# FFN1 of a transformer layer: sums of squares on TensorE, a scale on ScalarE, six g buffers, five chunks and adaLN dots placed one by one

## The chip, the cores and the metric

The kernel runs on one core of a Trainium2 chip. A core has five engines that run at the same time, each through its own queue in order: TensorE (PE in the profile), which multiplies matrices into PSUM; VectorE (DVE), ScalarE (ACT) and GpSimd (POOL), which work on vectors; and SyncE (SP), which issues the DMAs here. Engines wait for one another by semaphores. SBUF holds operands, 128 partitions wide; PSUM has eight banks of 512 float32 columns. The metric is the device time of one execution in microseconds (us), as the median of several runs.

## The reference

One layer of a diffusion transformer works on 512 latent and 256 context tokens of width 1024: a first half-step feed-forward network (FFN1), a token mixer (latent attention and a gated MLP), and a second network (FFN2). Nine rows of modulation come from one product of silu(c) with a wide matrix (adaLN), once for latent tokens and once for context tokens.

```python
def rms_norm(x, w):
    xf = x.astype(jnp.float32)
    y = xf * lax.rsqrt(jnp.mean(xf * xf, axis=-1, keepdims=True) + EPS)
    return (y * w.astype(jnp.float32)).astype(x.dtype)

def modulate(h, shift, scale):
    return h * (1 + scale) + shift

def swiglu(h, w1, w3, w2):
    return (jax.nn.silu(h @ w1) * (h @ w3)) @ w2

def ffn_sublayer(h_in, shift, scale, gate, norm_w, w1, w3, w2):
    h = modulate(rms_norm(h_in, norm_w), shift, scale)
    return h_in + 0.5 * gate * swiglu(h, w1, w3, w2)

# in hybrid_layer; D_MODEL 1024, D_FF 2816
    mx = jnp.split((jax.nn.silu(c) @ w_ada + b_ada)[:, None, :], N_MOD, axis=-1)
    mc = jnp.split((jax.nn.silu(c_ctx) @ w_ada + b_ada)[None, None, :], N_MOD, axis=-1)
    x = ffn_sublayer(x, mx[0], mx[1], mx[2], norm1_w, ffn1_w1, ffn1_w3, ffn1_w2)
    ctx = ffn_sublayer(ctx, mc[0], mc[1], mc[2], norm1_w, ffn1_w1, ffn1_w3, ffn1_w2)
```

## The kernel before

**Layout.** x lies transposed: 128 partitions, 8 slices k of the width, and 768 token columns, which are two halves of 256 latent and 128 context tokens. GA and GB are those halves of 384 columns. All float32 products are done with operands split into a high part (`oph`, `hh`, `gh`: a copy on ScalarE) and a low part (`opl`, `hl`, `gl`: a subtraction on VectorE), and three matmuls (L125 to L127: high by high, high by low, low by high). Every weight tile of 128x512 thus costs one copy and one subtraction (L102, L103).

**Start.** ScalarE squares x slice by slice (`square0`). VectorE adds the eight latent squares up (`add_sq`), one float32 matmul with a matrix of ones (L402) sums over partitions, and the inverse root follows (`rstd_start`, `rstd_end`). Before it, PE broadcasts silu(c) for both kinds of tokens into two double banks (L391, 32 passes), runs four matmuls with constants (L394, `WARM`), and ScalarE copies the broadcasts to `cb` (`put_cb`). The eight context squares are added on GpSimd and summed by L479.

**First loop, k = 0 to 7.** With `nc.ordered` set each engine keeps the order in which the code is written. A pass makes slice k of h: `first_x` (x times scale and inverse root, VectorE), `first_h` (adds the shift and makes the high part, ScalarE), `first_l` (low part, VectorE); in the same pass PE accumulates the up products of f = 0 and 1 for the latent columns (L441) and, some passes later, for the context columns (L434). Two adaLN rows are made on the way: scale by PE (`ada_row` L253, `ada_col` L260), shift by VectorE's dots (`ada_shift`).

**adaLN dots.** The other seven rows are dots on VectorE: 128x1024 weights times `cb`, with an accumulator (L223). There are 80 of them: 48 whose products go to a throw-away tile `junk` (two dots to each loaded half block, latent and context) and 32 which write over the half block (`raw`, one dot each). The throw-away tile shares its buffers (tag s1, two of them) with GpSimd's sum `s1` of each Winograd step. `ada_half` makes all the dots of a half block at once; `ada_step` calls it four times after f = 2 and after f = 3 and three times in each Winograd step, until they are used up.

**FFN1's f loop.** f = 2 and 3 are plain products (`up1`). Then the operands of a Strassen-Winograd scheme are made (blocks T1 to T4), and f = 4 to 21 need seven block products each (`head`, `mid`, `tail`), 84 matmuls of 384 columns. GpSimd makes sums of weights (L571 to L587). The results gh, gl of one f (`g_tile`) are kept until a chunk of them goes through the down product: `after1` calls `down` for the chunks of CHUNKS1, at set values of f, and VectorE adds each result bank, gated, to x (`evac_x` L319, one for the latent and one for the context columns). The last chunk (`last_down`) goes first for GA and then for GB, with the next norm between them.

**What sets the order.** Outside the pinned loop a scheduler that simulates the engines sets the order of each engine's instructions; buffers (three `raw`, two `block` tiles, five operand pairs, g tiles) limit how far work runs ahead. PSUM has two double banks (`big`) and four single ones (`mm`); a Winograd f takes four banks, alternately of one kind and the other, and `down` uses single ones. SyncE issues the loads of all weights in program order.

## Time and profile before

| | us |
|---|---|
| median of three runs | 1217.53 (1213.57 to 1220.31) |
| profiled execution | 1216.12 |
| its span | 1214.0 |
| first matmul of the first loop (L441) starts | 19.79 |
| last split of the first loop's last slice (`hl`, k = 7) starts | 69.68 |
| evacuation of the first down product begins | 150.9 |
| last down product's matmuls of FFN1 end | 593.0 |

The profile counts each engine's busy time; a matmul's busy time includes its pipeline, so that matmuls that follow at 0.17 us each have 0.34 us. A row of the timeline gives start, duration, engine, line, operation and tiles, and in brackets how long the engine had been idle and which instruction ended that. A row of the groups gives line, engine, tiles and shapes, the count, then busy time and mean ns of one, then the idle time before them by releaser. L57 is the wrapper through which the pinned stretch issues its work. "PEclk" is the clock that TensorE was granted, as a share of the full one.

### The profile page before, as it was taken

To read this page: it belongs to the slowest core of one execution; us is meant where nothing else is said; L and a number is where in the kernel's file an instruction comes from. 1 tells how busy PE (TensorE), PEld (TensorE's weight loads), DVE (VectorE), ACT (ScalarE), POOL (GpSimd) and SP (SyncE) were. 2 spreads that over 40 slices of the span, in tenths; PEclk is the share of its full clock that TensorE was granted. 3 is DMA by queue.
4 is the path that set the end of the run, shared out by engine and by line. 5 is a ranking of instruction groups with operands and counts; after the bars stand their busy time and mean duration, and the time that the engine had idled before them with its cause. 6 is when DMAs were issued, how large, how long until landed. Compare 5 with 4: busy or idle time off the path is not lost.

```text
span 1214.0 us, 18922 instructions
## 1 busy us (share of the span) xinstructions
PE 1149.2 (95%) x7042; PEld 1078.5 (89%) x7042; DVE 963.5 (79%) x1699; ACT 545.4 (45%) x1090; POOL 422.6 (35%) x388
## 2 busy tenths in 40 slices
PE   8899799979999999999999999998989999999998
PEld 5689699979999999998888789987888989899997
DVE  7999987897876977667864978759996879787784
ACT  6463312233143143245554549985653535354441
POOL 1102311222032042114426727885761424243320
PEclk9999999989999999999999999998999999999999
DMA  9434343343623723224221220003122332323302
GB/s 335 168 125 155 133 145 104 105 170 108 225 75 115 227 75 129 72 87 138 76 100 59 99 66 5 1 1 122 53 71 104 105 105 99 111 73 136 105 35 87
DMA packets 35514, 130.60 MB, mean 108 GB/s; under 512 B 3680, under 2 KB 10592, under 8 KB 29536
## 3 DMA queue, kind: packets, MB, share of 16 engines
q1 hardware_dynamic: 35280, 129.35, 31.3%
q8 instruction: 55, 0.90, 0.3%
q14 instruction: 35, 0.29, 0.1%
q10 hardware_dynamic: 144, 0.06, 0.0%
HBM read 127.30 MB, written 2.10 MB: 107 GB/s over the span
## 4 chain that ended last, share of the span: by engine, by line
PE 70%; DVE 14%; ACT 3%; issue 2%; DMA 1%; POOL 0%; DVEq 0%; POOLq 0%; ACTq 0%
PE mm L125 15%; PE mm L126 15%; PE mm L127 15%; PE big L125 7%; PE big L126 7%; PE big L127 7%; DVE opl L103 4%; DVE junk L223 1%; PE mm L1064 1%; DMA raw<-wada 1%; DVE x L319 1%; DVE hh L301 1%; PE mm L1079 1%; PE mm L1080 1%; DVE hl L302 1%
## 5 line engine op out<-in xcount | busy, mean ns | idle before, releaser
L102 ACT CAST oph<-block 128x512 fp32r<-128x512 f32 x228 | 141.3, 621 | 250.8 <-PE mm L126 167.2
L103 DVE TENSOR_TENSOR opl<-block,oph 128x512 fp32r<-128x512 f32 x228 | 209.3, 922 | 36.4 <-ACT oph L102 35.6
L125 PE MATMUL mm<-gh,oph 128*128 128x384 f32 (+2 forms) x532 | 187.4, 354 | 4.5 <-DVE x L319 4.0
L127 PE MATMUL mm<-gh,opl 128*128 128x384 f32 (+2 forms) x532 | 186.7, 353 | 4.6 <-DVE opl L103 4.6
L126 PE MATMUL mm<-gl,oph 128*128 128x384 f32 (+2 forms) x532 | 187.5, 352 | 0.0
L102 ACT CAST oph<-raw 128x512 fp32r<-128x512 f32 x154 | 94.0, 619 | 145.4 <-PE mm L126 87.1
L587 POOL TENSOR_TENSOR block<-block 128x512 f32<-128x512 f32 x38 | 51.6, 1357 | 258.3 <-DVE opl L103 231.0
L103 DVE TENSOR_TENSOR opl<-raw,oph 128x512 fp32r<-128x512 f32 x154 | 119.2, 779 | 19.6 <-ACT oph L102 19.4
L571 POOL TENSOR_TENSOR s<-block 128x512 f32<-128x512 f32 x38 | 54.7, 1440 | 197.6 <-DVE g L248 75.8
L125 PEld LDWEIGHTS mm<-gh,oph 128*128 128x128 f32 x532 | 100.2, 189 | 12.4 <-issue 4.4
L127 PEld LDWEIGHTS mm<-gh,opl 128*128 128x128 f32 x532 | 100.2, 189 | 12.0 <-DVE opl L103 5.2
L126 PEld LDWEIGHTS mm<-gl,oph 128*128 128x128 f32 x532 | 100.2, 188 | 6.6
L586 POOL TENSOR_TENSOR block<-s,block 128x512 f32<-128x512 f32 x38 | 54.4, 1432 | 121.4 <-DVE opl L103 120.8
L319 DVE SCALAR_TENSOR_TENSOR x<-mm,g,x 128x256 f32<-128x256 f32 x206 | 76.5, 413 | 19.1 <-PE mm L127 19.1
L125 PE MATMUL big<-hh,oph 128*128 128x384 f32 (+1 forms) x240 | 79.8, 333 | 9.6 <-DVE gl L306 7.9
L325 DVE SCALAR_TENSOR_TENSOR x<-mm,g,x 128x512 f32<-128x512 f32 x55 | 41.0, 748 | 50.6 <-PE mm L127 50.4
L126 PE MATMUL big<-hl,oph 128*128 128x384 f32 (+1 forms) x240 | 79.8, 333 | 0.0
L127 PE MATMUL big<-hh,opl 128*128 128x384 f32 (+1 forms) x240 | 79.6, 332 | 0.0
L223 DVE SCALAR_TENSOR_TENSOR junk<-raw,cb 128x1024 bf16<-128x1024 f32 x48 | 63.1, 1315 | 1.7 <-DMA raw<-wada 1.3
L585 POOL TENSOR_TENSOR block<-block 128x512 f32<-128x512 f32 x38 | 60.3, 1588 | 2.8
L127 PE MATMUL mm<-hh,opl 128*128 128x384 f32 x160 | 54.0, 337 | 3.0 <-DVE opl L103 3.0
L126 PE MATMUL mm<-hl,oph 128*128 128x384 f32 x160 | 54.6, 341 | 2.2 <-DVE hl L302 2.2
(500 smaller groups left out, 3390.5 us busy)
## 6 DMA issues: line engine op xcount, KB each, us to landing
raw<-wst SPq DMA_DIRECT2D x82, 512.0 KB, 3.7
block<-wst SPq DMA_DIRECT2D x38, 1024.0 KB, 4.9
raw<-wada SPq DMA_DIRECT2D x56, 512.0 KB, 4.4
block<-wada SPq DMA_DIRECT2D x8, 1024.0 KB, 6.3
x<-xT SPq DMA_DIRECT2D x6, 512.0 KB, 6.7
raw<-wfirst SPq DMA_DIRECT2D x8, 256.0 KB, 5.4
out<-x SPq DMA_DIRECT2D x7, 256.0 KB, 2.2
raw<-wuq SPq DMA_DIRECT2D x2, 384.0 KB, 3.1
```

The costliest lines, as they stand in the source:

```text
L102: self.nc.scalar.copy(dst[0], src)
L103: (eng or self.nc.vector).tensor_sub(dst[1], src, dst[0].bitcast(F32))
L125: nc.tensor.matmul(out, lh, rh, start=first, stop=False, skip_group_check=more)
L126: nc.tensor.matmul(out, lh, rl, start=False, stop=False, skip_group_check=more)
L127: nc.tensor.matmul(out, ll, rh, start=False, stop=last, skip_group_check=more)
L223: nc.vector.scalar_tensor_tensor(out, raw, 1.0, cb[:, which, :], ALU.mult, ALU.mult, accum_out=acc[which][:, c : c + 1] if to is None else to,
L319: nc.vector.scalar_tensor_tensor(x[:, dt, s0 : s0 + sn], pt[:, o : o + sn], mod_g[i][which][:, dt : dt + 1], x[:, dt, s0 : s0 + sn], ALU.m ...
L325: nc.vector.scalar_tensor_tensor(lat(x, dt), two(pt), mod_g[i][0][:, dt : dt + 1], lat(x, dt), ALU.mult, ALU.add)
L571: nc.gpsimd.tensor_add(s1, q[2], q[3])
L585: nc.gpsimd.tensor_sub(q[2], q[0], q[2])
L586: nc.gpsimd.tensor_sub(q[0], s1, q[0])
L587: nc.gpsimd.tensor_sub(q[1], q[1], q[0])
```

## The change

Five edits, all in FFN1:

1. Both sums of squares are accumulated on TensorE, eight float32 matmuls each (`sums`), in place of seven additions on VectorE or GpSimd and one matmul. The four constant matmuls (`WARM`) are gone. The broadcast of c for the context tokens (`put_c(1)`) moves behind `ada_col(0)`, and ScalarE copies each broadcast in two halves.
2. `first_x` is a plain product; the scale is given to the activation in `first_h`.
3. The first loop's latent products use the four single banks, its context products and the small results a double bank each; plain f and Winograd f of FFN1 swap the kind of bank by parity (`in_bigs`), and the first half of the last down uses double banks.
4. Six pairs of g buffers instead of five, five chunks (4, 4, 4, 4, 6) instead of six, whose downs come after f = 5, 9, 13 and 17 instead of after f = 5, 6, 10, 14 and 18.
5. `ada_rest` gives out one dot at a time: four after f = 2 and after f = 3, two in each Winograd step, and eleven in each down, between the evacuations. The throw-away tile is one of its own. The gate's columns are finished one by one.

```diff
-CHUNKS1 = [3, 3, 4, 4, 3, 5]
+CHUNKS1 = [4, 4, 4, 4, 6]
...
+    junk = fp.tile([P, D], BF16, bufs=1, name="junk")
...
-    def ada_dot(raw, c, which, to=None):
...
+    def ada_dot(raw, which, to, last=False):
+        nc.vector.scalar_tensor_tensor(raw if last else junk, raw, 1.0, cb[:, which, :], ALU.mult, ALU.mult, accum_out=to)
...
-    def ada_half(i):
-        r = st.half(wada, i)
-        for which in (0, 1) if i < 5 * NK else (0,):
-            ada_dot(r, i, which)
-            if i % NK == NK - 1:
-                mod_final(i // NK, slice(0, NK), which)
+    def ada_rest():
+        for d in range(NK):
+            r = st.half(wada, 2 * NK + d)
+            for which in range(2):
+                ada_dot(r, which, accg[:, d, which : which + 1])
+                yield
+            nc.vector.tensor_scalar(pairs[0][2][:, d, :], accg[:, d, :], col[:, 2 * NK + d : 2 * NK + d + 1], 0.5, ALU.add, ALU.mult)
+        for i in range(3 * NK, 9 * NK):
+            r = st.half(wada, i)
+            for which in (0, 1) if i < 5 * NK else (0,):
+                ada_dot(r, which, acc[which][:, i : i + 1], i >= 5 * NK)
+                if i % NK == NK - 1:
+                    mod_final(i // NK, slice(0, NK), which)
+                yield
...
-        nc.vector.scalar_tensor_tensor(sel(hf, k), sel(x, k), mod_a[0][which][:, k : k + 1], two(rs[which]), ALU.mult, ALU.mult)
+        nc.vector.tensor_mul(sel(hf, k), sel(x, k), two(rs[which]))
...
-        nc.scalar.activation(sel(hf, k), sel(hf, k), AF.Identity, bias=mod_s[0][which][:, k : k + 1])
+        nc.scalar.activation(sel(hf, k), sel(hf, k), AF.Identity, bias=mod_s[0][which][:, k : k + 1], scale=mod_a[0][which][:, k : k + 1])
...
+    bb = [bigs(2), [mm(), mm()]]
+    pa, sumx = bigs(2)
...
+    def sums(which, sq, k):
+        n = parts[which][1]
+        pin(nc.tensor.matmul(sumx[:, :n], ones, sq, start=k == 0, stop=k == NK - 1))
+
+    put_c(0)
     for k in range(NK):
-        sa = add_sq(sa, k, square0(0, k), nc.vector)
...
+        sums(0, square0(0, k), k)
+    copy_c(0)
...
     ada_col(row, 0)
+    put_c(1)
...
-    pbs = bigs(4)
-    pcs = []
-    sx = None
+    pbs = [mm() for _ in range(2 * NFIRST)]
+    pcs = bigs(NFIRST)
...
         if k == 0:
+            sqx = [square0(1, j) for j in range(NK)]
+        if k == 1:
             for j in range(NK):
-                sx = add_sq(sx, j, square0(1, j), nc.gpsimd)
-        if k == 1:
-            sumx = mm()[:, :256]
-            pin(nc.tensor.matmul(sumx, ones, sx, start=True, stop=True))
+                sums(1, sqx[j], j)
...
-        pool, bufs = (gp, 3) if f % 5 < 3 else (gp2, 2)
+        pool = gp if f % 6 < 3 else gp2
...
-        pbs, banks = part or ({}, bigs(2 * len(groups)))
+        pbs, banks = part or ({}, [mm() for _ in range(2 * len(groups))] if f % 2 else bigs(2 * len(groups)))
...
-            bigs4 = bigs(4) if f % 2 else None
+            bigs4 = bigs(4) if f % 2 == self.in_bigs else None
...
+    def ada_step(n=1):
+        for _ in range(n):
+            next(ada, None)
 
     def after1(f):
         if f < NPLAIN1:
-            for _ in range(4):
-                ada_step()
+            ada_step(4)
         for ci, n in enumerate(CHUNKS1[:-1]):
-            if f == (5 if ci == 0 else (starts1[ci] + n + 1) // 2 * 2):
-                down(starts1[ci], n, U_DN1 + starts1[ci], [GA, GB], lambda pt, dt, g, gn: evac_x(pt, dt, seg_of(g // 384), 0))
+            if f == starts1[ci] + n + 1:
+                slot = 0
+
+                def ev(pt, dt, g, gn):
+                    nonlocal slot
+                    evac_x(pt, dt, seg_of(g // 384), 0)
+                    slot += 1
+                    ada_step(slot % 3 > 0)
+
+                down(starts1[ci], n, U_DN1 + starts1[ci], [GA, GB], ev)
...
-    Winograd(gp, 384, U_UP1, blocks, g_tile, 1).run(NPLAIN1, after1, ada_step)
+    Winograd(gp, 384, U_UP1, blocks, g_tile, 1, 0).run(NPLAIN1, after1, lambda i: ada_step(i < 2))
```

More of the change, by code (lines that the diff above doesn't have):

```diff
@@ L35 @@
 RAWS = 3
-WARM = 4
 OPS = 5
@@ L160, in layer_kernel @@
     accs = const.tile([P, NK, 2], F32, name="accs")
+    accg = const.tile([P, NK, 2], F32, name="accg")
     epsc = const.tile([P, 1], F32, name="epsc")
@@ L414, in layer_kernel @@
     first_l(0, 0)
-    put_cb(1)
+    copy_c(1)
     for _ in shift:
@@ L488, in g_tile @@
     def g_tile(f):
[L489 to L490 removed]
+        pool = gp if f % 6 < 3 else gp2
+        gt[f] = tuple(pool.tile([P, 768], F32R, tag=t, bufs=3, name=f"{t}_{nc.next_id()}") for t in ("gh", "gl"))
         return gt[f]
@@ L518, in up1, with down @@
         return pbs, banks
-    def down(f0, n, u0, groups, evac, dts=range(NK), cache=None):
+    def down(f0, n, u0, groups, evac, dts=range(NK), cache=None, bank=None):
         us = {} if cache is None else cache
@@ L523, in down @@
             for g, gn in groups:
-                pt = mm()
+                pt = bank() if bank else mm()
                 for fi in range(n):
@@ L612, in tail, with run @@
             g_split(Z, gh[:, n:], gl[:, n:])
-        def run(self, f0, after, step=lambda: None):
+        def run(self, f0, after, step=lambda i: None):
             hd = self.head(f0)
@@ L718, in ev @@
             sa.add(dt, g0)
-        down(starts1[-1], CHUNKS1[-1], U_DN1 + starts1[-1], [(GA, GB)[g]], ev, dts, caches[g])
+        down(starts1[-1], CHUNKS1[-1], U_DN1 + starts1[-1], [(GA, GB)[g]], ev, dts, caches[g], None if g else lambda: last_banks.pop(0))
     sA, sB = SsqAcc(npool, 384, nc.gpsimd), SsqAcc(npool, 384, nc.vector)
     nc.scalar.activation(epsc2, gt[NF - 1][0][:, 767:768].bitcast(F32), AF.Abs_reciprocal_sqrt, bias=epsc, scale=0.0)
+    last_banks = [b for _ in range(4) for b in bigs(2)]
     last_down(0, sA, range(8))
+    assert next(ada, None) is None
     def normA():
@@ L1279, in layer_kernel @@
     blocks = {"B11": B11, "B21": B21, "B22": B22, "T1": T1, "T2": T2, "T3": T3, "T4": T4}
-    Winograd(f2, 256, U_UP2, blocks, g2_tile, 2).run(NPLAIN2, after2)
+    Winograd(f2, 256, U_UP2, blocks, g2_tile, 2, 1).run(NPLAIN2, after2)
     lastu = {}
```

54 lines of the change are left out of this document (14 added, 40 removed).

## The prediction

> **What bounds the kernel now.** The page first: TensorE (PE) is busy for 95% of the span, so an edit to FFN1 gains only where PE stands still inside FFN1. The windows of 20 us show where. A stretch at full rate holds 117 matmuls of 384 columns, 0.171 us apart.
>
> ```profile
> span 1214.0 us, 18922 instructions
> PE 1149.2 (95%) x7042; PEld 1078.5 (89%) x7042; DVE 963.5 (79%) x1699; ACT 545.4 (45%) x1090; POOL 422.6 (35%) x388
> ...
> 20.00:40.00 20.00, 14.61 (x71) 10.55 (x71) 19.72 (x34) 8.31 (x19) 8.87 (x7) 0.91 0.78 292
> ...
> 60.00:80.00 20.00, 18.40 (x106) 15.15 (x106) 19.36 (x40) 15.18 (x31) 0.00 (x0) 1.00 0.43 148
> 80.00:100.00 20.00, 19.10 (x114) 18.78 (x113) 19.63 (x38) 7.65 (x16) 0.00 (x0) 1.00 0.41 134
> 100.00:120.00 20.00, 18.52 (x107) 18.20 (x107) 19.37 (x32) 6.93 (x14) 6.00 (x4) 1.00 0.47 157
> 120.00:140.00 20.00, 17.18 (x96) 16.23 (x95) 20.00 (x29) 6.30 (x11) 7.62 (x5) 1.00 0.37 127
> 140.00:160.00 20.00, 14.72 (x66) 13.76 (x65) 18.17 (x31) 4.24 (x10) 4.07 (x3) 0.83 0.44 163
> 160.00:180.00 20.00, 20.00 (x117) 20.00 (x116) 19.03 (x42) 4.90 (x9) 4.88 (x3) 1.00 0.33 107
> ...
> 200.00:220.00 20.00, 18.54 (x107) 18.25 (x106) 18.81 (x41) 4.43 (x8) 4.21 (x3) 1.00 0.32 106
> ...
> 240.00:260.00 20.00, 12.13 (x59) 11.81 (x59) 20.00 (x32) 4.51 (x10) 6.92 (x5) 0.79 0.56 202
> 260.00:280.00 20.00, 20.00 (x112) 20.00 (x112) 15.12 (x25) 8.27 (x16) 5.48 (x4) 0.96 0.32 106
> ...
> 480.00:500.00 20.00, 18.48 (x106) 17.90 (x105) 14.79 (x37) 4.06 (x8) 1.29 (x1) 1.00 0.34 114
> ...
> 300.00:480.00 180.00, 180.00 (x1040) 180.00 (x1039) 143.04 (x259) 58.23 (x108) 45.81 (x32) 1.00 0.43 139
> ```
>
> Columns: stretch, length, PE, PE loads, VectorE (DVE), ScalarE, GpSimd (POOL), then granted clock. Where PE's count falls, DVE is at 18 to 20 of 20 us: from 60 to 160 and from 240 to 260 DVE is the bound. From 300 to 480 PE runs without a gap, so nothing is to be had there. The two long waits and the chain into the second:
>
> ```profile
> 149.86 0.69 PE L127 MATMUL mm<-gh,opl 128*128 128x384 f32 x1 [3.19 <-DVE opl L103]
> 150.35 0.52 PE L125 MATMUL mm<-gh,oph 128*128 128x384 f32 x1
> 150.67 0.52 PE L126 MATMUL mm<-gl,oph 128*128 128x384 f32 x1
> ...
> 256.00 0.69 PE L125 MATMUL big<-hh,oph 128*128 128x384 f32 x1 [7.87 <-DVE gl L306]
> ...
> 240.32 1.78 DVE junk L223 x2
> ...
> 243.23 1.22 DVE junk L223 x2
> 244.45 2.23 DVE raw L223 x2
> ...
> 253.87 1.14 DVE raw L223 x2
> 255.01 0.48 DVE big L611
> 255.49 0.47 DVE gl L306
> ```
>
> What delays PE is a bunch of adaLN dots (L223) put ahead of a split that PE needs. After each wait matmuls start 0.32 us apart, and the granted clock of those stretches is 0.83 and 0.79.
>
> **The change, part by part.** The rows that price it:
>
> ```profile
> 8.45 1.89 PE L394 MATMUL mm<-ones 128*128 128x256 f32 x8
> 11.96 1.12 PE L402 MATMUL mm<-sq,ones 128*128 128x512 f32 x2 [1.62 <-DVE sq L57]
> 13.02 1.14 PE L253 MATMUL mm<-block,sc 128*2 128x128 f32 x9
> 26.54 9.34 POOL L57 TENSOR_TENSOR sq<-sq,sq 128x256 f32<-128x256 f32 x7 [25.25 <-ACT sq L57]
> 25.93 0.68 DVE L57 TENSOR_TENSOR hl<-hfull,hh 128x512 fp32r<-128x512 f32 x1
> 26.53 1.22 DVE L57 SCALAR_TENSOR_TENSOR junk<-block,cb 128x1024 bf16<-128x1024 f32 x1
> 32.44 1.20 DVE L57 TENSOR_TENSOR hl<-hfull,hh 128x512 fp32r<-128x512 f32 x1
> 33.56 1.74 DVE L57 SCALAR_TENSOR_TENSOR junk<-block,cb 128x1024 bf16<-128x1024 f32 x1
> 35.93 0.70 PE L479 MATMUL mm<-sq,ones 128*128 128x256 f32 x2 [3.90 <-POOL sq L57]
> L223 DVE SCALAR_TENSOR_TENSOR raw<-raw,cb 128x1024 f32<-128x1024 f32 x25 | 32.5, 1301 | 6.4 <-DMA raw<-wada 6.1
> L319 DVE SCALAR_TENSOR_TENSOR x<-mm,g,x 128x256 f32<-128x256 f32 x96 | 45.8, 477 | 12.2 <-PE mm L127 12.2
> L319 DVE SCALAR_TENSOR_TENSOR x<-mm,g,x 128x128 f32<-128x128 f32 x96 | 32.6, 339 | 0.0
> raw<-wada SPq DMA_DIRECT2D x56, 512.0 KB, 4.4
> ```
>
> *Latent sums.* One float32 matmul is two records. L402's take 13.02 − 11.96 = 1.06 us a sum; L394's, with 256 columns, start about 0.21 apart, so 0.43 at 512 and 0.86 a sum. Half of the 32 broadcast passes now stand ahead, so the eight sums can start near 6.5 us and end at 13.4 (0.86) or 15.0 (1.06), against 13.02; they cannot end before the last square, at 11 us, plus one sum, 11.9. So −1.1 to +2.0; I take **+0.5**, since PE goes from one to the next as in L394. The Trainium skill (FP8 and Floating Point Precision, TensorE Precision Notes) has true FP32 as four passes through the array, and TensorE: Matmul & The Clock Gate, Part 1, 215.7 ns between warm matmuls of 512 columns: an estimate of 0.86 us a sum. By the pages this term is +0.5, by L402 alone it is +2.0; L394 agrees with the pages, and no run here shows sums in a row.
>
> *Context sums.* While POOL adds (26.54 to 35.88), DVE's subtract takes 1.20 instead of 0.68 and its dot 1.74 instead of 1.22: some 0.5 us on each of five, 2.5 in all. PE stands 3.90 us for POOL's sum. Instead PE gets 16 records at 0.21, 3.4 us, in pass k=1, just where it waited: it starts the third pass at 31 + 3.4 = 34.4 instead of 36.28, so −1.9. With DVE's 2.5 passed on in full, a little more. Range 0 to −4; I take **−2.5**. first_x loses its scale (about 0.07 us on each of 16, on DVE), which ScalarE's activation takes in at no added instruction; ScalarE is busy for 8 to 15 of 20 us there and has the cover. Without that cover it would cost as many tenths.
>
> *Up to the first down (60 to 160).* Missing matmuls there are 3 + 10 + 21 + 51 = 85 from 80 to 160, 14.5 us, and 1.6 in 60 to 80: 16.1 lost. In the new order f=2's products start already inside the last pass of the first loop, in their own banks:
>
> On PE, end of the first loop after the change (big_742 is the bank of f=2, mm_250 one of the first loop's last pass); before, all of that pass stood ahead of f=2:
> ```order
> L125 MATMUL big_742<-hl,oph_749 128x384
> L126 MATMUL big_742<-hh,opl_751 128x384
> L124 MATMUL big_742<-hh,oph_749 128x384
> L125 MATMUL big_742<-hl,oph_749 128x384
> L443 MATMUL mm_250<-hh,oph_628 128x512
> L126 MATMUL big_742<-hh,opl_751 128x384
> L124 MATMUL big_742<-hh,oph_749 128x384
> ```
> Some 13 matmuls, 2.2 us, are done before PE needs DVE's last split. From that split to the operand of the Y product of f=4, where DVE last holds PE in the new order, DVE has 15 dots (1.22 each, 18.3), 10 weight splits (0.68, 6.8), 16 block splits (0.55, 8.8) and some 30 smaller operations (0.42, 12.6): 46.5 us, an estimate from rows. PE has 231 matmuls there, 39.0 us: 7.5 lost. Gain 16.1 − 7.5 + 2.2 = **−11**, between 0 (DVE's order gives it back) and −16.
>
> *Dots spread singly (200 to 280).* Missing matmuls: 10 + 58 + 5 = 73, 12.5 us, half-rate stretches included. DVE's order at the end of f=6, before:
> ```order
> L223 SCALAR_TENSOR_TENSOR raw_2851,accc<-raw_2851,cb 128x1024
> L605 TENSOR_TENSOR big_1991<-big_1991,u_2389_2390 128x384
> L103 TENSOR_TENSOR opl_2666<-block_2424,oph_2664 128x512
> L223 SCALAR_TENSOR_TENSOR junk_2806,accc<-raw_2803,cb 128x1024
> L609 TENSOR_TENSOR big_1989<-big_1989,u_2389_2390 128x384
> L606 TENSOR_TENSOR big_1991<-big_1991,sl_2369 128x384
> L103 TENSOR_TENSOR opl_2688<-block_2424,oph_2686 128x512
> L223 SCALAR_TENSOR_TENSOR raw_2904,accc<-raw_2904,cb 128x1024
> ```
> and in the same place (the tail of a Winograd f, L604 to L610 being the former L605 to L611) after, f=6:
> ```order
> L604 TENSOR_TENSOR big_1436<-big_1436,u_1910_1911 128x384
> L102 TENSOR_TENSOR opl_2152<-block_1937,oph_2150 128x512
> L605 TENSOR_TENSOR big_1436<-big_1436,sl_1890 128x384
> L608 TENSOR_TENSOR big_1434<-big_1434,u_1910_1911 128x384
> L102 TENSOR_TENSOR opl_2174<-block_1937,oph_2172 128x512
> L309 TENSOR_TENSOR gl_1978<-big_1436,gh_1976 128x384
> ```
> The dots have left the tail; they stand between the evacuations of a down instead. A down of four is 192 matmuls, 33 us; DVE then has 16 × (0.477 + 0.339) = 13.1 us of evacuation, 11 dots at 1.22, 13.4, and 8 splits at 0.68, 5.4: 32 us, with no room for the neighbouring f's work. What DVE falls behind there shows in f=6, where six more dots stand ahead of the tail: I leave 4 us of the 12.5. So **−8.5**, between −12.5 and 0.
>
> *Five chunks, six g buffers, banks.* 480 to 500 misses 11 matmuls, 1.9 us, at a change of stage; a last chunk of six gives each group's evacuation 18 × 0.171 = 3.1 us of PE as cover instead of 2.6. I take **−3** for this and the norm behind it, from +1 (a bank that waits for its evacuation, which PE's next product otherwise hides) to −5. The same weights are loaded, in as many loads. Single banks, the shared junk tile and the gate columns taken one by one (eight operations of a few tenths, in DVE's 46.5) I cost at nothing more.
>
> *Sum:* 0.5 − 2.5 − 11 − 8.5 − 3 = −24.5. Against the profiled run's own 1216.1 that is 1191.6; the median shown is 1.4 higher, so about **1192** beside it (1193.0, less a rounding the terms do not support).
>
> **The rivals.**
> - *Dots wait for their loads* (slower). A load lands 4.4 us after its issue, and three raw buffers also carry down's weights. In the first two downs 4 + 5.5 loads go through them in 33 us, one per 3.5 us, against (4.4 + 4) / 3 = 2.8 if a pair of dots, split by an evacuation, holds its buffer for 4 us. In the last two each dot has a load of its own: 15 loads, one per 2.2 us, against (4.4 + 1.5) / 3 = 2.0. 44 dots stand inside the downs, and DVE has no room there, so each wait is PE's: above 24.5 / 44 = 0.56 us per dot the change loses; at 0.7 it ends at 1192 + 31 = 1223. Against it: 25 such dots from 300 to 480 waited 6.1 us, 0.24 each, and PE lost nothing. 8%.
> - *DVE stays the bound up to the first down*: the order pulls other DVE work forward, and the 11 us are not gained: 1203. 20.00 of 20 us from 120 to 140 speaks for it; 15 dots there instead of 26 against. 12%.
> - *The stall of 248 moves* behind the first down at full size: 1192 + 8.5 = 1200. DVE's 32 of 33 us speaks for it. 13%. Part of it is the clock: after 3.19 us of idling matmuls stood 0.32 us apart for 6 us, some 3 us lost. The Trainium skill (TensorE: Matmul & The Clock Gate, Part 1) lets the clock fall only after an idle window of about 3.4 us: by it a remainder of 3 us would cost no clock and the time would be 1197 instead of 1200; the row at 149.86 disagrees, and the row decides.
> - *All of DVE's stalls go*: −16 and −12.5 instead of −11 and −8.5: 1183. 14%.
> - *The change does not do what it says*: the scheduler, which sets the order, puts dots in pairs again as in f=6; that is the third rival's place and price.
>
> **How the numbers follow.** The forecast, 1186 to 1198, has 48%; the rivals in their order 8, 12, 13 and 14%; the last 5% is small mishaps together, around 1212. Range 1180 to 1208: it holds the forecast and rivals two to four but for a part of the last. Half a per cent, 6 us, is about what can be told from no change. Faster 0.89 (forecast, rivals two to four, 2 of the 5%), same 0.03 (the other 3 of it), slower 0.08 (the first rival).
>
> **What would show it.** In the changed profile: 16 records of sums in pass k=1 and DVE's subtract at 0.68 there; PE's counts from 100 to 160 near 110, none at 66; no wait near 8 us at the end of f=6, and granted clock 1.00 from 200 to 280; dots (L221) with under 0.3 us of idle ahead of them, and PE without waits for evacuations inside downs. It is wrong if PE waits for DVE throughout the four downs, or if a stretch that was full from 300 to 480 shows gaps.

## The result and the profile after

The changed kernel takes 1218.78 us (median of 20 runs, 1215.69 to 1222.08) against 1217.55 for the kernel before: 1.0015 times as long, 95% interval 1.0005 to 1.0024. Forecast were 1192. The profiles show one execution each, of 1220.65 us after and 1216.12 before, so the traces lie 3 us further apart than the medians. The 26 us that were to be gained are not there, although much of what was to bring them did happen, as the windows of 20 us of the changed kernel show.

```profile
span 1218.9 us, 18886 instructions
PE 1161.7 (95%) x7062; PEld 1087.3 (89%) x7062; DVE 947.9 (78%) x1666; ACT 547.3 (45%) x1094; POOL 412.4 (34%) x381
...
100.00:120.00 20.00, 18.19 (x105) 17.87 (x104) 19.93 (x33) 7.48 (x15) 6.89 (x4) 1.00 0.40 138
120.00:140.00 20.00, 17.83 (x93) 17.62 (x94) 18.75 (x30) 7.62 (x15) 6.66 (x5) 0.91 0.35 113
140.00:160.00 20.00, 19.88 (x115) 19.59 (x114) 16.42 (x30) 8.39 (x16) 4.21 (x3) 1.00 0.41 129
...
200.00:220.00 20.00, 17.76 (x99) 17.15 (x100) 19.83 (x30) 6.68 (x14) 11.98 (x7) 1.00 0.31 106
240.00:260.00 20.00, 19.40 (x112) 19.11 (x112) 16.65 (x33) 6.42 (x12) 3.09 (x2) 1.00 0.47 159
280.00:300.00 20.00, 18.08 (x96) 17.76 (x95) 14.97 (x25) 5.22 (x9) 5.42 (x4) 0.91 0.52 176
340.00:360.00 20.00, 16.80 (x89) 16.48 (x89) 14.04 (x27) 4.72 (x9) 2.93 (x2) 0.91 0.49 161
440.00:460.00 20.00, 16.98 (x90) 16.66 (x89) 14.00 (x27) 4.71 (x9) 3.05 (x2) 0.91 0.52 176
...
300.00:480.00 180.00, 170.34 (x958) 168.46 (x957) 137.23 (x253) 55.02 (x103) 40.49 (x28) 0.98 0.42 140
```

The stretch from 140 to 160 has 115 matmuls instead of 66, that from 240 to 260 has 112 instead of 59. But from 300 to 480, where TensorE (PE) had no gap before, 82 of 1040 matmuls are missing, and VectorE (DVE) is not full there: 14 of 20 us in the two worst stretches. Both traces can be laid side by side by the time at which PE starts its n-th matmul of 384 columns (worked out from the two traces, in us; differences of the unrounded times):

| n | before | after | difference |
|---|---|---|---|
| first matmul of the first loop | 19.8 | 25.1 | +5.3 |
| 100 (f = 2) | 97.2 | 100.0 | +2.8 |
| 400 (first down) | 163.5 | 158.4 | −5.2 |
| 1000 (past f = 6) | 280.2 | 266.5 | −13.7 |
| 1500 | 367.0 | 361.8 | −5.1 |
| 2100 | 471.0 | 475.2 | +4.2 |
| 2761 (last one of FFN1's last down) | 590.9 | 595.4 | +4.5 |

(In the table of times before, two entries differ from the trace: the first evacuation begins at 152.9, not 150.9, and the last down's matmuls end at 591.3, not 593.0.)

The change gains 19 us from the first matmul to n = 1000 and gives 18 back by n = 2100. What happens there is seen at the head of the down after f = 13. The timeline of the changed kernel, by queue (SyncE's issues, DVE, PE):

```profile
345.39 0.33 SPq L97 DMA_DIRECT2D raw<-wada  x1
...
345.28 0.08 DVE L221 DVE_READ_ACCUMULATOR raw<-raw,cb 128x1 f32 x1
346.35 0.55 DVE L605 TENSOR_TENSOR mm<-mm,sl 128x384 f32<-128x384 f32 x1
349.41 1.22 DVE L221 SCALAR_TENSOR_TENSOR raw<-raw,cb 128x1024 f32<-128x1024 f32 x1 [2.51 <-DMA raw<-wada]
350.56 0.56 DVE L608 TENSOR_TENSOR mm<-mm,u 128x384 f32<-128x384 f32 x1
351.43 0.55 DVE L309 TENSOR_TENSOR gl<-mm,gh 128x384 fp32r<-128x384 f32 x1
...
348.49 0.34 PE L126 MATMUL mm<-gh,opl 128*128 128x384 f32 x1
352.03 0.69 PE L124 MATMUL mm<-gh,oph 128*128 128x384 f32 x1 [3.20 <-DVE gl L309]
352.51 0.53 PE L125 MATMUL mm<-gl,oph 128*128 128x384 f32 x1
```

A dot ends at 345.36 and frees a raw buffer; the load of another dot is issued at 345.39, 0.03 us later; that dot starts at 349.41, after DVE stood idle for 2.51 us. Behind it in DVE's queue are the last operations of f = 13 (L608, then L309, which reads the bank of its result), and the down's next product needs that bank: PE waits 3.20 us and then matmuls start 0.32 us apart for a while. This dot is the 58th that DVE runs; the program gives out 50 ahead of this down and 11 between its evacuations. So it is one of the down's own dots, which DVE's order has ahead of its place, in the tail of f = 13. The groups show the same over all of FFN1, first before, then after; idle time for loads rises from 1.3 and 7.5 us to 8.0 and 18.4:

```profile
L223 DVE SCALAR_TENSOR_TENSOR junk<-raw,cb 128x1024 bf16<-128x1024 f32 x48 | 63.1, 1315 | 1.7 <-DMA raw<-wada 1.3
L223 DVE SCALAR_TENSOR_TENSOR raw<-raw,cb 128x1024 f32<-128x1024 f32 x32 | 42.7, 1335 | 7.8 <-DMA raw<-wada 7.5
...
L221 DVE SCALAR_TENSOR_TENSOR junk<-raw,cb 128x1024 bf16<-128x1024 f32 x48 | 60.7, 1265 | 8.1 <-DMA raw<-wada 8.0
L221 DVE SCALAR_TENSOR_TENSOR raw<-raw,cb 128x1024 f32<-128x1024 f32 x32 | 42.9, 1340 | 18.7 <-DMA raw<-wada 18.4
```

The second surprise is the start. Timeline of PE, ScalarE and DVE in the changed kernel:

```profile
4.51 3.75 PE L389 MATMUL big<-ident,sc 128*128 128x128 f32 x16 [0.54 <-ACT sc L217]
8.05 8.12 PE L398 MATMUL big<-sq,ones 128*128 128x512 f32 x16
16.95 1.91 PE L248 MATMUL big<-block,sc 128*2 128x128 f32 x16 [0.78 <-ACT r L56]
25.09 0.50 PE L443 MATMUL mm<-hh,oph 128*128 128x512 f32 x1
...
18.90 0.25 ACT L56 COPY row<-big 2x128 f32<-2x128 f32 x1 [2.00 <-PE big L248]
...
19.18 0.69 DVE L56 SCALAR_TENSOR_TENSOR v<-big,r 128x512 f32<-128x512 f32 x1 [2.50 <-ACT row L56]
```

The sums end at 16.2, and DVE's first step of the inverse root (`v<-big,r`) then stands 2.50 us for ScalarE's copy of the adaLN row, which has nothing to do with it but lies in the other half of the same double bank.

### The profile page after: what moved, and what is told of

It reads as the page before. It is cut to its first block, busy times and chain, and to the rows that moved or that the text cites. A ratio compares the mean times of both kernels' runs of the same rounds, so it can differ in the third digit from the quotient of the medians.

```text
span 1218.9 us, 18886 instructions
## 1 busy us (share of the span) xinstructions
PE 1161.7 (95%) x7062; PEld 1087.3 (89%) x7062; DVE 947.9 (78%) x1666; ACT 547.3 (45%) x1094; POOL 412.4 (34%) x381
## 4 chain that ended last, share of the span: by engine, by line
PE 66%; DVE 20%; DMA 6%; ACT 4%; issue 4%; POOL 0%; DVEq 0%; POOLq 0%; ACTq 0%
PE mm L124 13%; PE mm L125 13%; PE mm L126 12%; PE big L124 7%; PE big L125 7%; PE big L126 7%; DMA raw<-wada 5%; DVE opl L102 5%; DVE junk L221 2%; DVE x L322 2%; DVE raw L221 2%; PE mm L1070 1%; PE big L398 1%; PE mm L443 1%; DVE hl L305 1%
## 5 line engine op out<-in xcount | busy, mean ns | idle before, releaser
L124 PE MATMUL mm<-gh,oph 128*128 128x384 f32 (+2 forms) x484 | 172.4, 357 | 6.9 <-DVE gl L309 6.2
L125 PE MATMUL mm<-gl,oph 128*128 128x384 f32 (+2 forms) x484 | 172.2, 356 | 0.0
L126 PE MATMUL mm<-gh,opl 128*128 128x384 f32 (+2 forms) x484 | 171.3, 355 | 0.0
L586 POOL TENSOR_TENSOR block<-block 128x512 f32<-128x512 f32 x38 | 51.7, 1361 | 307.1 <-DVE opl L102 303.7
L102 DVE TENSOR_TENSOR opl<-raw,oph 128x512 fp32r<-128x512 f32 x156 | 120.8, 777 | 25.6 <-ACT oph L101 25.3
L322 DVE SCALAR_TENSOR_TENSOR x<-mm,g,x 128x256 f32<-128x256 f32 (+1 forms) x158 | 59.4, 414 | 20.1 <-PE mm L126 20.1
L124 PE MATMUL big<-hh,oph 128*128 128x384 f32 (+1 forms) x208 | 68.2, 328 | 3.2 <-DVE gl L309 3.2
L125 PE MATMUL big<-hl,oph 128*128 128x384 f32 (+1 forms) x208 | 68.2, 328 | 0.0
L126 PE MATMUL big<-hh,opl 128*128 128x384 f32 (+1 forms) x208 | 67.8, 326 | 0.0
L125 PE MATMUL mm<-hl,oph 128*128 128x384 f32 x192 | 65.1, 339 | 1.1 <-DVE hl L305 1.1
L124 PE MATMUL mm<-hh,oph 128*128 128x384 f32 x192 | 64.8, 337 | 1.0 <-DVE hh L304 0.7
```

The source lines that it names most:

```text
L102: (eng or self.nc.vector).tensor_sub(dst[1], src, dst[0].bitcast(F32))
L124: nc.tensor.matmul(out, lh, rh, start=first, stop=False, skip_group_check=more)
L125: nc.tensor.matmul(out, lh, rl, start=False, stop=False, skip_group_check=more)
L126: nc.tensor.matmul(out, ll, rh, start=False, stop=last, skip_group_check=more)
L322: nc.vector.scalar_tensor_tensor(x[:, dt, s0 : s0 + sn], pt[:, o : o + sn], mod_g[i][which][:, dt : dt + 1], x[:, dt, s0 : s0 + sn], ALU.m ...
L586: nc.gpsimd.tensor_sub(q[1], q[1], q[0])
```

## The experiments

Ratios are to the kernel before, run beside it on the same chip; the change itself stands at 1.0015. Lines of a run come from one of its executions.

**A bank of its own for the latent sums.**

```diff
     pa, sumx = bigs(2)
+    sum_bank = [mm(), sumx]
...
-        pin(nc.tensor.matmul(sumx[:, :n], ones, sq, start=k == 0, stop=k == NK - 1))
+        pin(nc.tensor.matmul(sum_bank[which][:, :n], ones, sq, start=k == 0, stop=k == NK - 1))
```

> The changed kernel with the latent sums in a single bank of their own. Theory (a false dependency through the shared double bank: the first step of the inverse root, which reads the sums, stands 2.50 us for ScalarE's copy of the adaLN row, and the row's matmuls stand for ScalarE's read of the sums): the first loop's first matmul moves from 25.09 to about 22.8, the whole by -2 us, to about 1217. Rival (the start is late only because the sums themselves end late): under 0.5 us, 1218.5 to 1219.

Measured 1216.72 us, ratio 0.9991 (0.9976 to 1.0006). Timeline of PE and DVE of this run:

```profile
6.45 7.03 PE L399 MATMUL mm<-sq,ones 128*128 128x512 f32 x16
20.51 0.50 PE L444 MATMUL mm<-hh,oph 128*128 128x512 f32 x1
...
14.24 0.69 DVE L56 SCALAR_TENSOR_TENSOR v<-mm,r 128x512 f32<-128x512 f32 x1 [0.24 <-ACT r L56]
```

The wait is 0.24 us instead of 2.50. Not all of the way from 25.09 to 20.51 is the bank's: another run with the shared bank (the one with downs after even f, below) has its first matmul at 22.75. What differs is when the small load of the columns lands: silu(c) starts at 4.14 us in the profile of the change and at 3.25 in that other run, and where it is late the broadcast passes and the first sums are slower. From the end of the sums to the first matmul it is 8.9 us in both of these (25.09 − 16.17 and 22.75 − 13.84) and 7.0 with the bank of its own (20.51 − 13.48). So the bank costs 1.9 us, near the 2 expected. In the time alone it is hardly clear of the noise: the interval touches that of the change (1.0005 to 1.0024).

**The old start, first loop and banks.** The first-loop code, the bank parity and the single banks of the last down's first half are put back as before; scale on ScalarE, g buffers, chunks and single dots stay.

```diff
-    bb = [bigs(2), [mm(), mm()]]
-    pa, sumx = bigs(2)
+    pa = mm()
+    bb = [big() for _ in range(2)]
...
-    pbs = [mm() for _ in range(2 * NFIRST)]
-    pcs = bigs(NFIRST)
+    pbs = bigs(4)
+    pcs = []
...
-    Winograd(gp, 384, U_UP1, blocks, g_tile, 1, 0).run(...)
+    Winograd(gp, 384, U_UP1, blocks, g_tile, 1, 1).run(...)
...
-    last_banks = [b for _ in range(4) for b in bigs(2)]
```

> The changed kernel with the start, the sums, the first loop's banks and the bank parity of before; the scale on ScalarE, the six g buffers, the chunks and the single dots stay. Theory (the start costs 5.3 us and the context sums bring little): first matmul of the first loop at 19.5 to 20, the whole -3 to -5, 1214 to 1216. Rival (the sums on TensorE gain in the first loop what they lose at the start): 1218 to 1220, and the stop for the context sum near 32 is back with 4 us.

Measured 1207.42 us, ratio 0.9919 (0.9893 to 0.9945): some 11 us below the change and below both expectations, so more than the start. Groups and one window of this run:

```profile
L222 DVE SCALAR_TENSOR_TENSOR raw<-raw,cb 128x1024 f32<-128x1024 f32 x32 | 42.0, 1314 | 18.3 <-DMA raw<-wada 18.0
...
300.00:480.00 180.00, 174.54 (x995) 171.71 (x994) 136.28 (x259) 56.16 (x105) 43.07 (x30) 1.00 0.43 140
```

DVE waits for its loads as long as in the change (18.0 against 18.4 us), and yet PE does 995 matmuls in that stretch instead of 958. So how much of a late dot's wait reaches PE depends on the banks. Some of it does in any case: before, the stretch had 1040. The earlier start (19.60 against 25.09) is no part of the gain in this trace: at n = 1000 the run stands at 267.5 us, the change at 266.5. Another 5 us come from the last down (see the table further below).

**Dots in the downs without loads.** Dots issued inside a down read a resident tile.

```diff
+    def ada_src(i):
+        return cb[:, 0, :] if resident[0] else st.half(wada, i)
...
-            r = st.half(wada, i)
+            r, own = ada_src(i), not resident[0]
...
+                    resident[0] = True
                     ada_step(slot % 3 > 0)
+                    resident[0] = False
```

> The changed kernel where dots issued inside the four downs read a tile that is already in SBUF in place of a loaded half block, so these dots have no load; their results are then not the layer's modulation. Same number of dots of the same size. Theory (dots in the downs wait for their loads, and VectorE's queue with them): the waits of TensorE near 291, 348, 391 to 410 and 450 go, some 15 us, 1202 to 1207. Rival (VectorE simply has too much to do in a down): the waits stay, 1215 to 1219.

Measured 1205.17 us, ratio 0.9894 (0.9870 to 0.9919), 14 us below the change. Timeline of PE and windows of this run:

```profile
306.47 0.47 PE L124 MATMUL big<-hh,oph 128*128 128x384 f32 x1 [4.55 <-DVE gl L314]
...
340.00:360.00 20.00, 20.00 (x117) 20.00 (x116) 15.63 (x34) 5.33 (x11) 2.58 (x2) 1.00 0.52 176
440.00:460.00 20.00, 20.00 (x117) 20.00 (x117) 11.73 (x28) 3.58 (x6) 1.29 (x1) 1.00 0.16 55
```

Both stretches are full. But the run does not change the loads alone: DVE runs the 44 dots as soon as it can, all between 110 and 327 us, and none of them stands in these two stretches. So it does not show that VectorE has the time for them in a down. Near 300 us, where they crowd, DVE is busy for 20.00 of 20 us from 280 to 320 and PE waits 4.55 us for a split behind them. What it does show: without waits for loads ahead of the tails of f = 13 and 17, PE has no long wait there.

**Dots of pairs in the downs.** Two dots to one load stand in the downs, dots with a load of their own in the Winograd steps.

```diff
-    ada = ada_rest()
+    pairs_it, singles_it = ada_pairs(), ada_singles()
...
+    def ada_wino(i):
+        early = wino_n[0] < 2 * 3
+        wino_n[0] += 1
+        ada_step(i < 2, not early)
```

> The changed kernel with the dots split in two kinds: in f = 2 to 5 and in the downs only dots of pairs (one load for two dots), in the Winograd steps from f = 6 only dots with a load of their own, two to each f. Number, size and spread of the dots as in the change. Theory (loads): the last two downs issue 5.5 loads for dots in place of 11 each, VectorE's waits for loads fall from 26 us to about 10 and the time to 1206 to 1211. Rival (VectorE's amount of work in the downs): no change, 1217 to 1220.

Measured 1208.33 us, ratio 0.9923 (0.9902 to 0.9944). Groups and window:

```profile
L221 DVE SCALAR_TENSOR_TENSOR junk<-raw,cb 128x1024 bf16<-128x1024 f32 x48 | 61.3, 1276 | 13.0 <-DMA raw<-wada 12.8
L221 DVE SCALAR_TENSOR_TENSOR raw<-raw,cb 128x1024 f32<-128x1024 f32 x32 | 40.2, 1255 | 8.8 <-DMA raw<-wada 8.4
...
300.00:480.00 180.00, 176.86 (x1018) 175.96 (x1017) 143.11 (x263) 57.52 (x107) 46.84 (x32) 1.00 0.39 125
```

The time falls as expected, the waits less than expected: 21 us of them are left, not 10, and fewer of them reach PE. In DVE's order the last two downs still hold 8 single-load dots each.

**The banks of before from f = 2 on**, with the first loop in single banks as in the change:

```diff
-        pbs, banks = part or ({}, [mm() for _ in range(2 * len(groups))] if f % 2 else bigs(2 * len(groups)))
+        pbs, banks = part or ({}, bigs(2 * len(groups)))
...
-    Winograd(gp, 384, U_UP1, blocks, g_tile, 1, 0).run(...)
+    Winograd(gp, 384, U_UP1, blocks, g_tile, 1, 1).run(...)
...
-    last_banks = [b for _ in range(4) for b in bigs(2)]
```

> The changed kernel with the first loop in single banks as in the change, but both plain f, the Winograd f and the last down in the kinds of bank of before. Theory (a down follows an odd f, whose four products the change put into the single banks that the down takes too, so the down's first matmul waits for VectorE's last reads of that f): the waits of 3.2 us at 348 and 449 go and PE's hits by late dots shrink, 1211 to 1214, with the late start (first matmul near 25) still there. Rival (the kind of bank is indifferent, the downs wait because the dots before them are late): 1217 to 1220.

Measured 1214.15 us (1208.15 to 1217.02; the profiled execution took 1209.69), ratio 0.9966 (0.9947 to 0.9985): at the upper edge of what was expected, by a sum that was not. The stretches 340:360 and 440:460 are full, but f = 3 now shares the double banks with f = 2 and waits there (timeline of PE):

```profile
96.49 0.66 PE L124 MATMUL big<-hh,oph 128*128 128x384 f32 x1 [8.31 <-DVE g L274]
...
340.00:360.00 20.00, 20.00 (x117) 19.96 (x116) 13.67 (x28) 5.70 (x11) 2.92 (x2) 1.00 0.55 184
440.00:460.00 20.00, 20.00 (x116) 19.77 (x116) 14.76 (x30) 5.49 (x11) 2.91 (x2) 1.00 0.55 171
```

**Old first loop and pairs together** (the second and the fourth run combined).

> Start, sums and all banks of before (as in the second run), and dots of pairs in the downs, single-load dots in the Winograd steps (as in the fourth). If the two losses are separate, their gains of 11 and 10 us add up: 1197 to 1200. If both only keep VectorE's late dots from reaching TensorE, they overlap: 1204 to 1207.

Measured 1206.44 us, ratio 0.9923 (0.9896 to 0.9951), no better than either alone (0.9919 and 0.9923). From n = 1000 to 2100 the losses overlap: one repair removes late dots, the other keeps them from PE, and the two together take 195.0 us there, pairs alone 195.4. The 5 us of the last down are gained too, but more is lost before n = 1000 (274.2, against 270.2 with pairs alone): the stretch from 200 to 220 has only 94 matmuls (99 in the change, 107 before). The profiled execution was the slowest of this run (1212.05), so the size of that loss is uncertain.

**The first part alone**: the kernel before with sums on TensorE, scale on ScalarE, single banks in the first loop, the other parity and double banks in the last down's first half.

> The kernel before with the first part of the change alone: sums on TensorE, scale on ScalarE, first loop in single banks, banks by the other parity; chunks, g buffers and bunches of dots as before. Theory: the start costs 5, the context sums and f = 2's products in the first loop give 3 to 5 back, and the first down, which follows an odd f, waits for banks: 1217 to 1223. Rival (the banks hurt only together with single dots): 1214 to 1217.

Measured 1221.41 us, ratio 1.0031 (1.0015 to 1.0047). This half of the change costs 4 us by itself. In its trace it stands level with the kernel before at n = 1000 (280.3 and 280.2); 3.4 us are lost between there and n = 2100 (194.2 against 190.8), and 3.4 more from n = 2300 to the end of FFN1, where the last down is (86.6 against 83.2).

**All three repairs on TensorE's sums**: bank of its own, banks of before from f = 2 on, pairs in the downs.

> The changed kernel with all three repairs: a bank of its own for the latent sums, the banks of before from f = 2 on, dots of pairs in the downs. Sums stay on TensorE and the first loop in single banks. If start (2), banks (6) and loads (10) are separate losses: 1199 to 1203. If the banks' and the loads' losses are one: 1204 to 1208.

Measured 1204.16 us, ratio 0.9896 (0.9867 to 0.9924), at the border of the two expectations; the wait of f = 3 for the double banks (8.3 us) is in it. The profiled execution, of 1199.72 us, was the fastest of this run.

**Downs after even f.** The down then stands beside an f whose products lie in double banks.

```diff
-            if f == starts1[ci] + n + 1:
+            if f == starts1[ci] + n:
```

> The changed kernel with each of the four downs one f earlier, after f = 4, 8, 12 and 16. Those f have their products in double banks there, the down keeps the single ones; banks, dots and start as in the change. Theory (a down waits for the banks of the f beside it, and passes VectorE's late dots on to TensorE): the 3.2 us waits at the head of the downs go, 1211 to 1214. Rival (loads alone decide): 1217 to 1220.

Measured 1209.10 us, ratio 0.9938 (0.9917 to 0.9958), a little under what was expected. Groups and first matmul of this run:

```profile
L221 DVE SCALAR_TENSOR_TENSOR raw<-raw,cb 128x1024 f32<-128x1024 f32 x32 | 40.2, 1258 | 21.8 <-DMA raw<-wada 21.8
...
22.75 0.50 PE L443 MATMUL mm<-hh,oph 128*128 128x512 f32 x1
```

The dots wait even longer for their loads (21.8 us), there is no wait of 3 us at the head of a down, and 9 us are gained, 6 of them between n = 1000 and n = 2100. With the second and the fifth run this shows the other half of the cause: a late dot delays the evacuation of the f beside the down, and where the down takes the same kind of bank, PE waits with it.

**Latent sums as before, in a bank of their own.**

```diff
     put_c(0)
+    put_c(1)
+    for i in range(4):
+        pin(nc.tensor.matmul(two(warm[:, :256]), ones, ones2, start=True, stop=True))
+    sa = None
     for k in range(NK):
-        sums(0, square0(0, k), k)
+        sq = square0(0, k)
+        if sa is None:
+            sa = sq
+        else:
+            nc.vector.tensor_add(sa, sa, sq)
...
+    pin(nc.tensor.matmul(sum_bank[0], ones, sa, start=True, stop=True))
```

> The changed kernel with the latent sums as before (additions on VectorE, both broadcasts and four constant matmuls ahead of one sum, here in a bank of its own); context sums on TensorE, first loop in single banks, everything later as in the change. Theory (start 5.3 us late: 3 from the sums at half clock and in a row, 2 from the shared bank): first matmul of the first loop near 19.8, 1213 to 1215, and some 2 to 3 below the run with the bank alone. Rival (VectorE bounds the first loop anyway): as the run with the bank alone, 1216 to 1217.

Measured 1217.05 us, ratio 1.0005 (0.9986 to 1.0025): not below the run with the bank alone (0.9991), and at the rival's figure. The theory's place is right and its size is not. First matmul, and a window at the fourth down:

```profile
19.55 0.50 PE L452 MATMUL mm<-hh,oph 128*128 128x512 f32 x1
...
440.00:460.00 20.00, 17.01 (x83) 16.69 (x82) 15.10 (x29) 3.75 (x8) 1.22 (x1) 0.83 0.44 137
```

The first loop starts at 19.55 against 20.51 with the bank alone: the eight sums on TensorE cost 1.0 us, not 3. (In the run below with everything repaired, which starts in the same way, it is 19.93, so 0.6.) The rival's reason does not hold either: past the first loop, at n = 1000, the microsecond is still there (263.5 against 264.7). It does not reach the end: the stretch 440:460 has 83 matmuls here, 89 there, and the single-load dots wait 20.5 us instead of 18.7. That an early start is eaten by longer waits for loads is read from these two traces alone; no run separates it from their scatter.

**Everything repaired**: latent sums as before in a bank of their own, downs after even f, pairs in the downs; first loop, context sums, g buffers and chunks of the change.

> The three repairs together, first loop in single banks and banks of the change: latent sums as before in a bank of their own, downs after even f, dots of pairs in the downs and single-load dots in the Winograd steps. If the losses are those named (start 5, loads 10, banks 6, the last two partly the same): 1198 to 1203. Rival (VectorE's work before the first down, now one f earlier, becomes the wait): 1204 to 1209.

Measured 1201.35 us (1197.98 to 1202.92), ratio 0.9873 (0.9846 to 0.9899): 1.3% faster than the kernel before, the best version here, and within what was expected. It still has the double banks in the last down. Window of this run:

```profile
300.00:480.00 180.00, 178.44 (x1025) 177.10 (x1024) 142.03 (x265) 59.46 (x110) 43.06 (x31) 1.00 0.41 134
```

**Dots in bunches.** The change with the dots given out as before.

```diff
-                    ada_step(slot % 3 > 0)
...
-    Winograd(gp, 384, U_UP1, blocks, g_tile, 1, 0).run(NPLAIN1, after1, lambda i: ada_step(i < 2))
+    Winograd(gp, 384, U_UP1, blocks, g_tile, 1, 0).run(NPLAIN1, after1, lambda i: ada_step())
```

> The changed kernel with the dots given out as before: all dots of a half block at once, four half blocks after f = 2 and 3, three in each Winograd step, none in the downs; the rest as in the change. Theory (single dots end the wait of 8 us at f = 6 but bring waits for loads later): the wait of some 8 us and the half clock come back before 260, and the gaps from 290 to 450 go: 1217 to 1222. Rival (bunches were not what delayed f = 6): 1207 to 1212.

Measured 1211.19 us, ratio 0.9954 (0.9937 to 0.9971): the time falls in the rival's range. Timeline, group and window of this run:

```profile
220.94 0.69 PE L124 MATMUL big<-hh,oph 128*128 128x384 f32 x1 [5.07 <-DVE gl L309]
...
L221 DVE SCALAR_TENSOR_TENSOR raw<-raw,cb 128x1024 f32<-128x1024 f32 x32 | 41.3, 1292 | 9.9 <-DMA raw<-wada 9.5
...
300.00:480.00 180.00, 180.00 (x1040) 179.91 (x1039) 133.56 (x247) 59.03 (x110) 45.31 (x32) 1.00 0.37 122
```

Both halves of the theory are seen, and the sizes go against it: the wait at the end of f = 6 is back with 5.07 us (7.87 before), and from 300 to 480 PE is full again. Single dots as the change has them cost 7 us more than the bunches they replace: they are 10.0 us ahead at n = 1000 (266.5 against 276.6) and lose 18.0 from there to n = 2100. What differs is not how many dots DVE runs during a down. The program puts none there in this run, but in DVE's order the downs that begin at 255 and 347 us have 12 and 11 in their time, between the evacuations. Before, those that begin at 290 and 382 us have 11 and 12; in the change it is 14 and 13.

## Why the prediction was wrong

The step that failed is the reading of DVE's order, "The dots have left the tail; they stand between the evacuations of a down instead", with a cost of nothing beyond DVE's own time. It was taken from one place, the end of f = 6, and loads that come late were a rival of 8%. At f = 13 and f = 17 two dots with loads of their own do stand in the tail, and from n = 1000 to n = 2100 the change loses 17.9 us that the sum did not have. The prediction's own sign came true: gaps in stretches that were full from 300 to 480.

Where a late dot stands decides. The table counts the dots from n = 1000 to 2100 for whose load DVE stood idle for over 0.2 us, by the operation behind them in DVE's queue: an evacuation of a down, or an operation of a Winograd f (a split, a sum, `gl`). All is worked out from the traces, one execution each, in us; the last column is the last down's first half, which has a chunk of five before and of six in the others:

| kernel | waits of dots ahead of an evacuation | ahead of an operation of a Winograd f | n = 1000 to 2100 | 2450 to 2600 |
|---|---|---|---|---|
| before | 6.0 | 0 | 190.8 | 29.0 |
| dots in bunches | 7.9 | 0 | 190.7 | 31.1 |
| no loads for dots of the downs | 2.7 | 0 | 198.2 | 31.3 |
| pairs in the downs | 4.6 | 4.8 | 195.4 | 32.5 |
| the change | 4.9 | 13.6 | 208.7 | 31.3 |
| downs after even f | 6.1 | 15.5 | 202.8 | 32.5 |
| old start, first loop and banks | 4.7 | 13.3 | 200.1 | 26.6 |
| banks of before from f = 2 on | 5.1 | 14.4 | 200.7 | 26.6 |
| old first loop and pairs | 6.8 | 5.3 | 195.0 | 26.6 |

Two more runs leave this part as the change has it (the bank of its own, and the latent sums as before); they wait 14.4 and 14.2 us ahead of a Winograd f and take 205.8 and 208.8, so some 3 us of a difference are scatter. Late dots ahead of evacuations cost PE nothing, before and with bunches. Late dots ahead of a Winograd f cost 15 to 18 us with the banks of the change: five of PE's six waits in the change follow one within 5 us, and these waits with the slow matmuls behind them are the whole loss. (What the run without loads loses is mostly the 4.55 us wait behind crowded dots.) The rival was right that loads would come late and wrong that each wait is PE's. It was given little because 25 single-load dots before had waited 0.24 us each without harm to PE. That row was read as a property of the dots, but it was one of their place: every late one stood ahead of an evacuation. Why the order of the change has its dots elsewhere was not settled.

The second failed step is the sentence that lets PE's next product hide every bank that waits for its evacuation. A down after an odd f takes, with the new parity, the kind of bank which that f still holds; this turns a late dot into a wait of PE. The kernel before had the same neighbourhood (its later downs follow even f, whose products were in single banks then), but no late dots ahead of that f's last operations. By the table, the same waits of dots (13 to 15 us) cost some 10 us with the banks of before, 12 with the downs after even f, and 15 to 18 with the change's. With bunches the banks of the change cost nothing there; with the chunks of before they cost 3.4 (the first part alone). So the two causes overlap, and their repairs do not add up there.

The same sentence fails in the last down, without any dots. Its first half takes double banks in the change, and the timeline of the change has PE wait there for an evacuation:

```profile
549.53 0.69 PE L124 MATMUL big<-gh,oph 128*128 128x384 f32 x1 [1.91 <-DVE x L322]
```

After it matmuls start 0.32 us apart until 552.90. In all nine kernels with the change's banks the matmuls from n = 2450 to 2600 take 31.1 to 32.5 us, in all four with the banks of before and the chunk of six 26.6. That is some 5 us for the banks; parity and double banks were always changed together, so which of the two it is was not settled.

The other terms, by the table of start times:

- *Latent sums, +0.5:* right in size; TensorE's eight sums cost 0.6 to 1.0 (20.51 against 19.93 and 19.55). What the term lacked is the double bank that the sums share with the adaLN rows, 1.9 us. The diff shows it (`pa, sumx = bigs(2)`), and it was missed. The rest of the 5.3 goes with the late landing of the columns in this profile, which is seen with the old start too: in the run with the old first loop and pairs, the broadcasts of silu(c) start at 4.66 and the first matmul at 21.67.
- *FP32 in four passes:* the prediction's estimate from the four passes of the Trainium skill (FP8 and Floating Point Precision, TensorE Precision Notes) was 0.86 us a sum, L402's row gave 1.06. Measured are 7.03 us for eight in a row, 0.88 each, so the estimate and L394 were the better guide. Where the columns land late it is 7.27 to 8.12 for the eight.
- *Context sums, −2.5, and up to the first down, −11:* from the first matmul to n = 400 the difference goes from +5.3 to −5.2, a gain of 10.5 where 13.5 were forecast. PE's count from 140 to 160 was to be near 110 and is 115; those from 100 to 140 stayed at 105 and 93, with a wait of 3.98 us for DVE. (In the term's sum, 231 matmuls were set at 39.0 us; at the pace of 1040 in 180 us they take 40.0.)
- *Dots spread singly (200 to 280), −8.5:* −5.2 at n = 400, −13.7 at n = 1000, so −8.5. Right, to the tenth by luck. The run with bunches shows that about half of this is not the spreading: without any single dots it takes 112.3 us from n = 400 to 1000, against 116.7 before and 108.2 in the change.
- *Chunks and buffers, −3:* the change of stage near 480 gave 2.1 as read; between 540 and 560 it lost 2.4 again. From n = 2100 to the end of FFN1 it is +0.3 (120.2 against 119.9). Two runs with the banks of before take 115.5: chunks and buffers did bring 4.4, and the banks took it back.
- *The clock rule:* after the wait of 3.20 us matmuls start 0.32 us apart until 354.75 (granted clock 0.91 in that window), and after one of 1.92 us they do so too:

```profile
293.23 0.45 PE L124 MATMUL big<-u3h,oph 128*128 128x384 f32 x1 [1.92 <-DVE u L591]
```

The Trainium skill's idle window of about 3.4 us (TensorE: Matmul & The Clock Gate, Part 1) would not have let the clock fall; as with the row at 149.86, the measurement decides. Other waits of that length, the one of 1.89 us at 212.35 for one, are followed by matmuls at full pace, so what decides stays open.

What stays open: whether a fourth raw buffer would do what the pairs do. It wasn't tried, and no run shows whether there is room for it beside the six g buffers. Nor was it settled what the single dots alone are worth in a kernel with the even downs, or what the best run would take with single banks in the last down.

## What to carry to other kernels

An instruction that waits for a load delays everything behind it in its queue. So before filler work is moved, read the engine's actual order at every place where the filler comes to stand, not at one, and name what stands behind each: here a late dot ahead of an evacuation cost nothing, and one ahead of a split that PE needed cost 3 us. The place in the program is no guide, since the order may pull a filler forward. A row that shows a wait doing no harm holds only where the row stands: ask what stood behind it, and whether the change puts something else there. Two banks of one allocation were waited for here as if they were one (2.50 us, and 0.24 with a bank of its own), so put what is written early and what is read late into separate ones.

## What was unexpected

The start has two forms, and they go with the landing of a small load. Where the broadcast passes begin at 4.5 us or later (the change, its first part alone, pairs in the downs, bunches), 16 of them take 3.75 us and the eight sums 7.27 to 8.12; where they begin at 3.75 or 4.12 (even downs, and the bank of its own), they take 3.21 or 2.50 and the sums 7.03. With the sums in the shared bank the first loop then begins about 2 us later (24.4 to 25.3 against 22.3 to 22.9), and so it did with the old start (21.67 against 19.60, broadcasts from 4.66 and 3.79), though there the first 16 passes were not slower (2.02 and 3.57 us). The granted clock of the first window reads 1.00 in the change all the same. Why the passes are slower is not shown.

While GpSimd runs twelve short operations, most of them on the rotary tables, from 540.47 to 544.5 us in the changed kernel, one subtraction of VectorE that takes 0.68 us elsewhere takes 4.12:

```profile
540.90 4.12 DVE L102 TENSOR_TENSOR opl<-raw,oph 128x512 fp32r<-128x512 f32 x1
...
542.76 1.01 POOL L711 TENSOR_TENSOR sinw<-raw 128x48 f32<-128x48 f32 x4
543.74 0.73 POOL L701 TENSOR_TENSOR kpw<-raw,kpw 128x256 fp32r<-128x256 f32 x1
```

It ends 0.55 us after the last of them ends, which looks as if GpSimd's operations went ahead of it one after the other. It is not what the change lost from 540 to 560: the kernel before has such a subtraction too (4.11 us from 550.44), and so has the run with the old start, first loop and banks (4.12 us from 536.19), where PE has no such loss.
